# Layer two's projections from scaled float16 halves, with the weights' scale found while layer one runs

## The chip, the cores and the metric

The kernel runs on one core of a Trainium2 chip. A core has engines that run side by side, each through its own list of instructions in order: TensorE (PE, with the load of its stationary operand shown as PEld), VectorE (DVE), ScalarE (ACT), GpSimd (POOL) and SyncE (SP), which here issues the DMA transfers. The metric is the device time of one execution, in microseconds.

## The reference

Two layers over 1024 tokens of width 1024, with 256 memory tokens. Cut to what matters:

```
h = x @ w_in                       # 1024 x 3072: main, memory queries, main gate, memory gate
y_main = main_fn(u_main)           # layer one: pooling in four groups; layer two: forgetting attention, 16 heads
y_mem  = memory_attention(q_mem)   # 4 heads into the memory tokens
y = concat([y_main * silu(g_main), y_mem * silu(g_mem)])
x = layer_norm(ALPHA * x + y @ w_out)
...
h = x @ w_kv_shared                # between the layers: keys, values and forget logits of the attention
logit[t,s] = q_t.k_s/sqrt(64) + cum[t] - cum[s], causal
```

All inputs and the output are float32.

## The kernel before

**Split products.** Every operand is kept as a high and a low part, and a product is three matmuls: high x high, and the two cross products (`three`). High parts are fp32r, which PE takes as f32; low parts are bf16, and so are the operands of both cross products. `hi_lo` makes the parts: ACT casts the high part (L189), DVE subtracts it to get the low one (L190), and a third copy gives the high part in bf16, unless it is read in place as every second bf16 of the f32 tile (`in_place`, L200 with its neighbours, used for weights).

**Slabs.** A projection is worked by `slab`: one slab is 1024 x 128 of a weight matrix, times x turned (width on the partitions), for all 1024 tokens. The weights come in two pieces of 128 x 512 (256 KB; SP loads them into `raw`, a ring of four buffers, and the parts go into rings of four, `w` and `wl`). There are two accumulators, one for each half of the tokens, in banks of a two-bank ring `pj`; for each, 8 products are high x high and 16 cross, 48 matmuls of 512 columns in all, at L253. Layer one has 24 slabs of w_in, layer two 24 of w_in, 8 of the keys and 6 of the values; the first values and the forget logits are 64 x 3 matmuls of 272 columns in `v_first`. The very first slab starts while x is still arriving: its weights are at hand (`ready`), and for each eighth of the width it takes both halves of the tokens in turn.

**Order of work.** PE's instructions are in the order of the program, written by hand. The other engines' lists are ordered by a scheduler. SP issues the transfers in the order of its list and waits at each for its buffer and for one of eight semaphores.

**Layer one.** Four pool groups (`pool_group`); the memory attention lies between group 0 and group 1. A group has two slabs for the values, window sums on DVE (L704 to L710), two slabs for the gates (ACT L283, DVE L284) and four short accumulations of six matmuls with the pool's own weights (PE L231) in a ring `L` of three banks. DVE's L736 multiplies each by its gate, and the result `Y` goes to DRAM (`y0d`).

**Output projection.** `OutProj.rest` takes the tokens in four steps of 256 (`sp`), each in three passes over a third of the mixed width (`c`): SP loads the third as `T` from `y0d`, ACT and DVE split it, PE does 48 matmuls at L540. After the third pass `norm` adds the residual (x rows into `G`), normalises and stores. `turned_rows` turns the rows for layer two: ACT scales them into float16 (hi), DVE gives the rest (lo), SP turns both with a DMA transpose, and ACT L351, DVE L352 and POOL L353 scale them back into f32 and bf16 parts.

**Layer two.** The memory attention and the attention loop `fox`: for each of the heads, 8 tiles of logits (PE L231, a group of three matmuls), DVE L986 adds the forget terms from `R` and takes the maximum, ACT the exponentials, PE the values. POOL masks the diagonal block of `R` ahead of DVE (the select, L978). PE's spare room is filled with the slabs of the pairs of heads to come (`Fill`). In this loop ACT and DVE are left the attention's work, and POOL splits the weights (`low`): L199 makes the high part, L200 the low one, for 54 pieces. `late_gate` does the gates of three pairs late: their slab runs in the loop, and then POOL multiplies the pair's result, loaded back into `R`, by the gate in four products (L1082) and SP stores it.

## Time and profile before

| | |
|---|---|
| median of 3 runs | 1200.42 us (1200.19 to 1201.05) |
| the profiled execution | 1202.12 us |
| its span | 1200.3 us |
| mean granted TensorE clock | 0.997 |
| PE busy | 1182.0 us, 98% |
| DVE, ACT, POOL busy | 800.9, 616.4, 208.3 us |
| DMA queue of the kernel | 180.81 MB, 61.9% of 16 engines' span |

The profile comes from one execution, whose own time stands beside its span; the runs were timed without it. Rows of groups read: line, engine, operation, result<-inputs by the program's names, shape, count | busy us, mean ns of one | idle time of the engine just before, and what ended it. Rows of a timeline begin with the start and the time busy in us. A matmul's end is modelled and overlaps the next one's start, so the time of a matmul in a stream is the distance of two starts, not its duration.

### The profile page before, as it was taken

How to read it: one execution, taken by the hardware profiler on the slowest of the kernel's cores; microseconds unless marked ns; L12 is line 12 of the kernel's file. 1: busy time of each engine (PE TensorE's matmuls, PEld its weight loads, DVE VectorE, ACT ScalarE, POOL GpSimd, SP SyncE). 2: the span in 40 equal slices, each digit the busy share in tenths (PEclk: the TensorE clock that was granted, in tenths of full speed). 3: DMA queues.
4: the chain of work that ended last, by engine and by line, in shares of the span. 5: the costliest groups of instructions: out<-in, count | busy, mean ns of one | idle time of the engine just before them, and what ended most of it. 6: DMA issues, size and time to landing. Idle time of an engine off the chain costs nothing. (4 is left out here: it accounts for less than half of the span.)

```text
span 1200.3 us, 19589 instructions
## 1 busy us (share of the span) xinstructions
PE 1182.0 (98%) x6927; PEld 739.8 (62%) x6927; DVE 800.9 (67%) x1864; ACT 616.4 (51%) x1330; POOL 208.3 (17%) x312
## 2 busy tenths in 40 slices
PE   9999999999999999999999999999999999999997
PEld 4566665555555555677776666666666666655554
DVE  6644766474656676377546888778878888784653
ACT  6433664261532224366325777767766787673110
POOL 2000000000000000200103334343334324530000
PEclk9999999999999999999999999999999999999999
DMA  6333654242265567355526789979997999977431
GB/s 237 110 102 89 137 118 152 85 123 80 92 206 158 158 150 167 106 133 103 173 54 158 153 196 175 194 157 192 189 183 169 192 199 202 228 199 230 157 113 49
DMA packets 280804, 182.06 MB, mean 152 GB/s; under 512 B 225025, under 2 KB 238977, under 8 KB 280705
## 3 DMA queue, kind: packets, MB, share of 16 engines
q1 hardware_dynamic: 280704, 180.81, 61.9%
q8 instruction: 54, 0.88, 0.3%
q14 instruction: 46, 0.37, 0.1%
HBM read 95.24 MB, written 22.61 MB: 98 GB/s over the span
## 5 line engine op out<-in xcount | busy, mean ns | idle before, releaser
L253 PE MATMUL pj<-A,w 128*128 128x512 bf16 (+1 forms) x1888 | 593.9, 398 | 2.7 <-ACT A L189 1.6
L253 PE MATMUL pj<-A,wl 128*128 128x512 bf16 x944 | 357.5, 380 | 0.0
L253 PEld LDWEIGHTS pj<-A,w 128*128 128x128 f32 x944 | 174.9, 189 | 46.5 <-ACT A L189 2.2
L253 PEld LDWEIGHTS <-w 128*128 128x128 bf16 x960 | 92.7, 98 | 120.4 <-issue 38.3
L253 PEld LDWEIGHTS <-wl 128*128 128x128 bf16 x960 | 94.3, 98 | 89.2 <-issue 4.8
L994 ACT ACTIVATE T<-MK,s 128x512 f32<-128x512 f32 x192 | 111.0, 578 | 46.7 <-DVE s L986 24.4
L1015 ACT ACTIVATE P<-T,s 128x512 f16<-128x512 f32 x192 | 102.9, 576 | 52.3 <-issue 25.8
L1016 DVE SCALAR_TENSOR_TENSOR P<-T,s,P 128x512 f16<-128x512 f32 x192 | 112.3, 612 | 24.0 <-ACT P L1015 22.3
L540 PEld LDWEIGHTS <-T 128*128 128x128 bf16 x736 | 70.6, 98 | 88.8 <-issue 6.5
L190 DVE TENSOR_TENSOR wl<-raw,w 128x512 bf16<-128x512 f32 (+1 forms) x96 | 67.8, 712 | 74.3 <-ACT w L189 71.6
L231 PE MATMUL L<-B,B 128*128 128x512 f32 (+3 forms) x384 | 109.2, 387 | 5.7 <-DVE s L986 5.3
L189 ACT CAST w<-raw 128x512 fp32r<-128x512 f32 (+1 forms) x104 | 62.8, 609 | 86.0 <-PE pj L253 64.7
L231 PEld LDWEIGHTS L<-B,B 128*128 128x128 f32 x384 | 71.1, 189 | 31.0 <-DVE s L986 11.3
L353 POOL TENSOR_SCALAR A<-A 128x1024 bf16<-128x1024 f32 x8 | 8.4, 1046 | 447.0 <-ACT A L351 430.3
L978 POOL TENSOR_SCALAR_AFFINE_SELECT R<-R 128x128 f32<-128x128 f32 x128 | 41.9, 333 | 210.0 <-DVE s L986 164.5
L986 DVE CUSTOM_DVE_ANT_0 MK<-L,R 128x512 f32<-128x512 f32 (+3 forms) x128 | 72.8, 568 | 8.0 <-PE L L231 5.6
L200 POOL TENSOR_TENSOR wl<-raw,w 128x512 bf16<-128x512 f32 x54 | 69.3, 1283 | 3.8
L190 DVE TENSOR_TENSOR T<-T,T 128x1024 bf16<-128x1024 f32 x23 | 31.7, 1378 | 46.1 <-ACT T L189 46.0
L189 ACT CAST T<-T 128x1024 fp32r<-128x1024 f32 x23 | 24.1, 1048 | 70.4 <-DMA T<-y1d 45.5
L199 POOL TENSOR_SCALAR w<-raw 128x512 fp32r<-128x512 f32 x54 | 35.7, 661 | 58.7 <-PE pj L253 58.7
L540 PE MATMUL L<-B,T 128*128 128x512 bf16 (+1 forms) x168 | 43.6, 391 | 0.0
L433 ACT ACTIVATE P<-L,s 128x256 f32<-128x256 f32 x64 | 29.6, 473 | 23.3 <-issue 13.0
(296 smaller groups left out, 1793.9 us busy)
## 6 DMA issues: line engine op xcount, KB each, us to landing
raw<-in_win_dram SPq DMA_DIRECT2D x94, 256.0 KB, 2.9
raw<-in_wout_dram SPq DMA_DIRECT2D x40, 256.0 KB, 3.0
B<-B SPq DMA_DIRECT2D x32, 256.0 KB, 4.6
R<-cumd SPq DMA_DIRECT2D x16, 512.0 KB, 4.5
T<-y0d SPq DMA_DIRECT2D x12, 512.0 KB, 4.8
y0d<-Y SPq DMA_DIRECT2D x11, 512.0 KB, 2.7
T<-y1d SPq DMA_DIRECT2D x11, 512.0 KB, 4.7
raw<-in_wmk_dram SPq DMA_DIRECT2D x16, 256.0 KB, 2.7
```

The costliest lines, as they stand in the source:

```text
L189: pin(nc.scalar.copy(hi, src))
L190: pin(by.tensor_tensor(lo[0], src, hi.bitcast(F32), ALU.subtract))
L199: nc.gpsimd.tensor_scalar(hi, src, 1.0, 1.0, ALU.mult, ALU.mult)
L200: nc.gpsimd.tensor_tensor(lo[0], src, hi.bitcast(F32), ALU.subtract)
L231: nc.tensor.matmul(acc, a, b, start=i == 0, stop=i == len(terms) - 1)
L253: nc.tensor.matmul(acc, a, b, start=start, stop=stop)
L540: nc.tensor.matmul(acc, y, w, start=c == 2 and j == firsts[id(acc)] and acc is not self.seeded, stop=c == 1 and j == lasts[id(acc)], skip_ ...
L978: nc.gpsimd.affine_select(R[:, qs], R[:, qs], [[-1, P]], ALU.is_ge, -NEG, base=0, channel_multiplier=1).ins
L986: nc.vector.tensor_tensor_reduce(p[:, lo:up], lg, R[:, lo:up], 1.0, top, ALU.add, ALU.min, m[:, n : n + 1])
L994: nc.scalar.activation(e, p[:, lo:up], AF.Exp, bias=top, scale=-1.0, accum_out=sums[:, n, hd % 2, i : i + 1],)
L1015: nc.scalar.activation(pair[:, lo:up], e, AF.Copy, scale=r)
L1016: nc.vector.scalar_tensor_tensor(pair[:, L + lo : L + up], e, r, pair[:, lo:up], ALU.mult, ALU.subtract)
```

## The change

Six parts, which belong together:

1. x of layer two is kept as two float16 halves (`Tiled`), scaled by a power of two, in blocks of 128 tokens; a slab's matmul takes four such blocks as its moving operand. `turned_rows` ends with the DMA transposes, which write the halves straight into place. L351, L352 and L353 are gone.
2. The weights of layer two's slabs and of `v_first` are scaled by one power of two and split into float16 halves (`split_f16`). All three matmuls of a product are float16. The scales are undone in the operations that empty the accumulators, which were there before.
3. The scale is found in layer one. `look_over` loads all 38 slabs (512 KB each) and the four pieces of `v_first` once more and takes the largest magnitude of each with one DVE reduction; 16 go through the ring `W` in the first two pool groups, 26 through eight slots of a buffer `A` that x of layer one leaves free, in `rest`. The maximum over the partitions goes through DRAM (`weight_scale`).
4. Where POOL splits weights, a multiplication by the scale (L226) comes ahead of the two operations (L227, L228).
5. The first slab takes the three products of the first half of the tokens, then those of the second, for the first two eighths of the width.
6. The four products of a late gate are queued (`lates`) and taken one per tile of logits, two per tile once the last head is under way.

```diff
+class Tiled:
+    def __init__(self, t):
+        self.t = t
+    def at(self, kt, cols):
+        a, b = cols.start // P, cols.stop // P
+        hi, lo = (self.t[:, e, a, kt, :] if b == a + 1 else self.t[:, e, a:b, kt, :] for e in range(2))
+        return hi, (lo, hi)
...
+    def split_f16(src, make):
+        t = make()
+        hi, lo = t[:, 0], t[:, 1]
+        if low[0]:
+            nc.gpsimd.tensor_tensor(src, src, wscale[0].to_broadcast([P, src.shape[1]]) if len(src.shape) == 2 else wscale[0].unsqueeze(2).to_broadcast(list(src.shape)), ALU.mult)
+            nc.gpsimd.tensor_scalar(hi, src, 1.0, 1.0, ALU.mult, ALU.mult)
+            nc.gpsimd.tensor_tensor(lo, src, hi, ALU.subtract)
+        else:
+            nc.scalar.activation(hi, src, AF.Copy, scale=wscale[0])
+            nc.vector.scalar_tensor_tensor(lo, src, wscale[0], hi, ALU.mult, ALU.subtract)
+        return hi, (lo, hi)
+    def w_f16():
+        return sb([P, 2, 4, P], "w", 4, F16)
+    def split_wide(src_dram, make):
+        r = raw([P, 4, P])
+        nc.sync.dma_start(r, src_dram)
+        return split_f16(r, make or w_f16)
...
+        split = split_wide if tiled else lambda src, make: split_w(src, [P, 4, P], make=make or wt)
...
+            nc.tensor.matmul(acc.rearrange("p (s t) -> p s t", t=P) if tiled else acc, a, b, start=start, stop=stop)
...
-                for i in range(3):
-                    for n in range(2):
-                        put(accs[n], *both[n][i], kt == 0 and i == 0, kt == KT - 1 and i == 2)
+                turns = [(i, n) for i in range(3) for n in range(2)]
+                for i, n in sorted(turns, key=lambda t: t[1]) if kt < 2 else turns:
...
+                    if look[0] and len(homes) < 2:
+                        seen[0] = acc
+                        next(look[0], None)
...
-    def turned_rows(z, rows, scale, XH, XL, half, whole):
-        sc, un = scale
-        hi, lo = (half() for _ in range(2))
-        nc.scalar.activation(hi, z, AF.Copy, scale=sc)
-        nc.vector.scalar_tensor_tensor(lo, z, sc, hi, ALU.mult, ALU.subtract)
-        t = whole()
-        nc.sync.dma_start_transpose(t[:, :KT, :], hi)
-        nc.sync.dma_start_transpose(t[:, KT:, :], lo)
-        nc.scalar.activation(XH[:, :, rows], t[:, :KT, :], AF.Copy, scale=un)
-        nc.vector.tensor_scalar(XL[0][:, :, rows], t[:, KT:, :], un, None, ALU.mult)
-        nc.gpsimd.tensor_scalar(XL[1][:, :, rows], XH[:, :, rows].bitcast(F32), 1.0, 1.0, ALU.mult, ALU.mult)
+    def turned_rows(z, tile_of, sc, X, half):
+        for e in range(2):
+            t = half()
+            if e == 0:
+                hi = t
+                nc.scalar.activation(hi, z, AF.Copy, scale=sc)
+            else:
+                nc.vector.scalar_tensor_tensor(t, z, sc, hi, ALU.mult, ALU.subtract)
+            nc.sync.dma_start_transpose(X.t[:, e, tile_of], t)
...
+    def look_over():
+        parts = [(win[1, n], 8 * P) for n in range(24)] + [(wk[n], 8 * P) for n in range(8)]
+        parts += [(wv[n], 8 * P) for n in range(6)] + [(wv0[n], 2 * FW) for n in range(4)]
+        landed = []
+        def reduced():
+            n, t = landed.pop(0)
+            nc.vector.tensor_reduce(tops[:, n : n + 1], t, AX.X, ALU.max, apply_absolute_value=True)
+        for n, (src, cols) in enumerate(parts):
+            t = homes[-1]()[:, :cols]
+            if n < 4:
+                nc.scalar.copy(t[:, :1], seen[0][:, :1])
+            if cols == 8 * P:
+                nc.sync.dma_start(t.rearrange("p (c k) -> p c k", c=2), src.rearrange("c p k m -> p c (k m)"))
+            else:
+                nc.sync.dma_start(t, src.rearrange("p k m -> p (k m)"))
+            landed.append((n, t))
+            if len(landed) > 2:
+                reduced()
+            yield
+        while landed:
+            reduced()
+        m = tiny(1)
+        nc.vector.tensor_reduce(m, tops[:, : len(parts)], AX.X, ALU.max)
+        nc.sync.dma_start(topd.rearrange("a p -> p a"), m)
...
+    def weight_scale():
+        row, m, e, sc = sb([P, P], "raw", 4), tiny(1), tiny(1), wscale[0][:, 6:7]
+        nc.sync.dma_start(row, topd[0].partition_broadcast(P))
+        nc.vector.tensor_reduce(m, row, AX.X, ALU.max)
+        nc.vector.tensor_scalar(m, m, 2.0 ** -100, None, ALU.max)
+        nc.vector.tensor_scalar(e.bitcast(I32), m.bitcast(I32), 0x7F800000, None, ALU.bitwise_and)
+        nc.vector.reciprocal(sc, e)
+        nc.vector.tensor_scalar(sc, sc, 2.0 ** 14, None, ALU.mult)
+        return e
...
+                if look[0] and sp == 3 and c == 2:
+                    run(look[0])
+                    look[0] = None
+                    scales(weight_scale())
...
+                if look[0] and sp < 3:
+                    for _ in range(4):
+                        next(look[0], None)
...
+            if g == 1:
+                homes.append(lambda: sb([P, S], "W", 4, F32, in0))
+                look[0] = look_over()
             pool_group(g)
+            if g == 2:
+                homes.append(None)
             out_proj.split((4, 12, 12)[g - 1])
-        XH1, XL1 = xs()
-        turns = out_proj.rest(x, XH1, XL1, x1)
+        X1 = Tiled(sb([P, 2, ST, KT, P], "A", 2, F16))
+        spare, turn_of = sb([P, 8, S], "A", 2), []
+        def aside():
+            turn_of.append(0)
+            return spare[:, len(turn_of) % 8]
+        homes.append(aside)
+        turns = out_proj.rest(x, X1, None, x1)
...
-            for c in range(4):
+            def product(c):
                 cols = slice(c * 2 * P, (c + 1) * 2 * P)
                 nc.gpsimd.tensor_tensor(o[:, cols], o[:, cols], g[:, cols], ALU.mult)
-            nc.sync.dma_start(y1d[pr // 4][:, pr % 4, :], o)
+                if c == 3:
+                    nc.sync.dma_start(y1d[pr // 4][:, pr % 4, :], o)
+            lates.extend((lambda c=c: product(c)) for c in range(4))
...
+                    for _ in range(min(1 if hd < HEADS else 2, len(lates))):
+                        lates.pop(0)()
```

DVE at the end of pool group 1, before (gates L284, splits of weights L190, evacuations L736):

```order
L190 TENSOR_TENSOR wl_2428<-raw_2425,w_2427 128x512 [waits DMAHW2_49,PE_49,Activation_49]
L190 TENSOR_TENSOR wl_2434<-raw_2431,w_2433 128x512 [waits DMAHW3_49,PE_49,Activation_49]
L284 SCALAR_TENSOR_TENSOR Y_2216<-Y_2216,pj_2256 128x512 [waits Activation_49]
L736 SCALAR_TENSOR_TENSOR Y_2149<-L_2283,pschalf,Y_2149 128x512 [waits DVE_49,PE_49]
L736 SCALAR_TENSOR_TENSOR Y_2149<-L_2291,pschalf,Y_2149 128x512 [waits DVE_49,PE_49]
```

And after (reductions L432 of looks in the ring `W`, splits L203, gate L324, evacuations L839):

```order
L432 TENSOR_REDUCE tops<-W_2497 128x1 [waits DMAHW7_49]
L432 TENSOR_REDUCE tops<-W_2526 128x1 [waits DMAHW0_49]
L203 TENSOR_TENSOR wl_2462<-raw_2459,w_2461 128x512 [waits DMAHW2_49,PE_49,Activation_49]
L432 TENSOR_REDUCE tops<-W_2593 128x1 [waits DMAHW2_49]
L324 SCALAR_TENSOR_TENSOR Y_2238<-Y_2238,pj_2281 128x512 [waits Activation_49]
L839 SCALAR_TENSOR_TENSOR Y_2165<-L_2311,pschalf,Y_2165 128x512 [waits PE_49]
L203 TENSOR_TENSOR wl_2468<-raw_2465,w_2467 128x512 [waits DMAHW5_49]
L839 SCALAR_TENSOR_TENSOR Y_2165<-L_2319,pschalf,Y_2165 128x512 [waits DVE_49,PE_49]
```

All 16 looks of the ring `W` have moved into this stretch; 13 of their reductions stand ahead of the first evacuation.

DVE at the beginning of the output projection, before: the last gate (L284), the four evacuations of the last pool group (L736), then the split of output weights. `Y` are the gated results, `L` the banks.

```order
L190 TENSOR_TENSOR wl_3083<-raw_3088,w_3080 128x512 [waits DMAHW7_49,PE_49]
L284 SCALAR_TENSOR_TENSOR Y_2974<-Y_2974,pj_3014 128x512 [waits Activation_49]
L736 SCALAR_TENSOR_TENSOR Y_2907<-L_3041,pschalf,Y_2907 128x512 [waits PE_49]
L736 SCALAR_TENSOR_TENSOR Y_2907<-L_3049,pschalf,Y_2907 128x512 [waits DVE_49,PE_49]
L736 SCALAR_TENSOR_TENSOR Y_2974<-L_3058,pschalf,Y_2974 128x512 [waits DVE_49,PE_49]
L736 SCALAR_TENSOR_TENSOR Y_2974<-L_3066,pschalf,Y_2974 128x512 [waits DVE_49,PE_49]
```

The same place after (gate L324, evacuation L839, reduction L432 of a look in buffer `A`):

```order
L203 TENSOR_TENSOR wl_3135<-raw_3140,w_3132 128x512 [waits DMAHW7_49,PE_49]
L432 TENSOR_REDUCE tops<-A_3128 128x1 [waits DMAHW6_49]
L324 SCALAR_TENSOR_TENSOR Y_3026<-Y_3026,pj_3066 128x512 [waits Activation_49]
L839 SCALAR_TENSOR_TENSOR Y_2959<-L_3093,pschalf,Y_2959 128x512 [waits PE_49]
L432 TENSOR_REDUCE tops<-A_3128 128x1 [waits DMAHW7_49]
L839 SCALAR_TENSOR_TENSOR Y_2959<-L_3101,pschalf,Y_2959 128x512 [waits DVE_49,PE_49]
L432 TENSOR_REDUCE tops<-A_3128 128x1 [waits DMAHW1_49]
L839 SCALAR_TENSOR_TENSOR Y_3026<-L_3110,pschalf,Y_3026 128x512 [waits DVE_49,PE_49]
```

One reduction, which waits for its load, stands ahead of the last gate, and two stand among the evacuations. SP at the same place, before and then after (L582 and L678 load `T`, L737 and L840 store `Y`, L439 is a look):

```order
L582 DMA T_3174<-y0d 128x4x256
L495 DMA raw_3124<-in_wout_dram 128x512
L737 DMA y0d<-Y_2907 128x1024
L582 DMA T_3227<-y0d 128x4x256
L737 DMA y0d<-Y_2974 128x1024
```

```order
L678 DMA T_3226<-y0d 128x4x256
L439 DMA A_3128<-in_win_dram 128x2x512 x2
L591 DMA raw_3176<-in_wout_dram 128x512
L439 DMA A_3128<-in_win_dram 128x2x512 x3
L840 DMA y0d<-Y_2959 128x1024
L678 DMA T_3287<-y0d 128x4x256
L840 DMA y0d<-Y_3026 128x1024
```

Five looks stand ahead of the first store and of the second load of `T`. POOL in the attention loop, before and then after, with the splits of two pieces between selects (L978, then L1096):

```order
L978 AFFINE_SELECT R_7322<-R_7322 128x128 [waits DMAHW3_49]
L199 TENSOR_SCALAR w_7746<-raw_7744 128x512 [waits DMAHW6_49,PE_49]
L200 TENSOR_TENSOR wl_7747<-raw_7744,w_7746 128x512 [waits PE_49,Pool_49]
L199 TENSOR_SCALAR w_7758<-raw_7756 128x512 [waits DMAHW1_49,PE_49]
L200 TENSOR_TENSOR wl_7759<-raw_7756,w_7758 128x512 [waits PE_49,Pool_49]
```

```order
L1096 AFFINE_SELECT R_7383<-R_7383 128x128 [waits DMAHW7_49]
L226 TENSOR_TENSOR raw_7931<-raw_7931,unrow 128x512 [waits DMAHW4_49,Pool_49]
L227 TENSOR_SCALAR w_7807<-raw_7805 128x512 [waits PE_49]
L228 TENSOR_TENSOR w_7807<-raw_7805,w_7807 128x512 [waits Pool_49]
L227 TENSOR_SCALAR w_7819<-raw_7817 128x512 [waits PE_49]
L228 TENSOR_TENSOR w_7819<-raw_7817,w_7819 128x512 [waits Pool_49]
L1096 AFFINE_SELECT R_7383<-R_7383 128x128 [waits DVE_49]
```

The multiplication of a piece to come (L226) now stands between a select and the two splits, and waits for that piece's load. POOL at the first late gate, before and then after:

```order
L1082 TENSOR_TENSOR R_11733<-R_11733,G_11734 128x256 [waits DMAHW2_49,DVE_49]
L1082 TENSOR_TENSOR R_11733<-R_11733,G_11734 128x256
L1082 TENSOR_TENSOR R_11733<-R_11733,G_11734 128x256 [waits DVE_49]
L1082 TENSOR_TENSOR R_11733<-R_11733,G_11734 128x256
L978 AFFINE_SELECT R_11630<-R_11630 128x128 [waits DVE_49] x3
```

```order
L1201 TENSOR_TENSOR R_11794<-R_11794,G_11795 128x256 [waits DMAHW6_49,DVE_49]
L1201 TENSOR_TENSOR R_11794<-R_11794,G_11795 128x256
L1096 AFFINE_SELECT R_11691<-R_11691 128x128 [waits DVE_49]
L1201 TENSOR_TENSOR R_11794<-R_11794,G_11795 128x256 x2
L1096 AFFINE_SELECT R_11691<-R_11691 128x128 [waits DVE_49] x2
```

A select now stands between the first two products and the last two.

97 lines of the change are left out of this document (60 added, 37 removed).

## The prediction

> **What bounds the kernel now.** I read the page's head, then the waits of PE, then the timeline and the windows at the places where the change takes work away or adds it.
>
> ```profile
> span 1200.3 us, 19589 instructions
> PE 1182.0 (98%) x6927; PEld 739.8 (62%) x6927; DVE 800.9 (67%) x1864; ACT 616.4 (51%) x1330; POOL 208.3 (17%) x312
> ```
>
> PE is busy for 98% of the span, the next engine for 67%. What PE waits for, by releaser (total, times, longest):
>
> ```profile
> PE L L231 <- DVE s L986: 5.3, 10, 1.1
> PE pj L253 <- ACT A L189: 1.6, 1, 1.6
> ```
>
> So there is nothing large to win by removing waits. Time comes down if matmuls get shorter, and goes up if a wait is created. ±2.4 us, 0.2%, is about what a measurement of this kernel can tell from no change.
>
> **Shorter matmuls (the gain).** A slab is 48 matmuls of 512 columns, 16 of them f32 and 32 of 16 bits. PE's timeline over two whole slabs of layer one (start, busy):
>
> ```profile
> 295.65 0.38 PE L253 MATMUL pj<-A,wl 128*128 128x512 bf16 x1
> 295.68 3.34 PE L253 MATMUL pj<-A,w 128*128 128x512 f32 x13
> 298.85 0.38 PE L253 MATMUL pj<-A,wl 128*128 128x512 bf16 x1
> ...
> 301.87 0.38 PE L253 MATMUL pj<-A,wl 128*128 128x512 bf16 x1
> 301.90 1.51 PE L253 MATMUL pj<-A,w 128*128 128x512 f32 x5
> 303.25 0.38 PE L253 MATMUL pj<-A,wl 128*128 128x512 bf16 x1
> ...
> 306.30 3.34 PE L253 MATMUL pj<-A,w 128*128 128x512 f32 x13
> ...
> 316.91 0.58 PE L253 MATMUL pj<-A,w 128*128 128x512 f32 x1
> ```
>
> The pattern repeats after 10.62 and 10.61 us, so a slab takes 10.615 us. From 298.85 to 301.87 there are 14 steps between bf16 starts: 0.2157 us each. 48 of those are 10.354 us, so f32 costs a slab 0.261 us. The two blocks confirm it: (3.20 - 0.216)/13 = 0.2295 and (1.38 - 0.216)/5 = 0.2328 us, which is 12 ns for each f32 matmul and some 25 ns for each block's borders. Float16 in the trace so far:
>
> ```profile
> 567.62 0.83 PE L231 MATMUL T<-T,MK 128*128 128x128 f16 x12
> L231 PE MATMUL T<-T,MK 128*128 128x128 f16 x288 | 20.1, 219 | 0.0
> ```
>
> (0.83 - 0.219)/11 = 55.5 ns for 128 columns, 222 ns for four times as many against 216: a float16 product is no slower than bf16. No row has a moving operand of four blocks of 128; I price it at the 216 of one block, with 222 as the dear end (38 x 48 x 6.3 ns = 11.5 us, more than the gain). 38 slabs x 0.261 = 9.9 us. The 64 f32 products of 272 columns in v_first give 64 x 14.5 ns x 272/512 = 0.5. Against that, in the attention loop the filler's f32 blocks (a third of its products) today often touch the f32 logits of L231; then all borders are open: 128 groups x 1/3 x 25 ns = 1.1 back. **Sum -9.3**, between -10.4 and, with four-block operands at 222 ns, +2.2.
>
> Removed beside PE: eight ACT copies L351, eight DVE scalings L352, eight POOL copies L353 in the turn of the rows. PE has no wait at the border of the layers, so I take 0.
>
> **First slab by halves of the tokens.** PE's start:
>
> ```profile
> 6.72 1.10 PE L253 MATMUL pj<-A,w 128*128 128x512 f32 x3 [1.61 <-ACT A L189]
> ```
>
> The 1.61 us wait is for ACT's half of x. Doing the three products of the first half ahead gives up to three matmuls (0.65 us) to fill it with, if their low halves are there. I take -0.3, from -0.65 to +0.3.
>
> **Late gate's products one per tile.** POOL's timeline, then PE's:
>
> ```profile
> 1036.83 2.81 POOL L1082 TENSOR_TENSOR R<-R,G 128x256 f32<-128x256 f32 x4 [2.23 <-DMA R<-y1d]
> 1039.59 0.29 POOL L978 TENSOR_SCALAR_AFFINE_SELECT R<-R 128x128 f32<-128x128 f32 x1
> 1044.14 0.50 PE L231 MATMUL L<-B,B 128*128 128x256 f32 x2 [1.12 <-DVE s L986]
> ```
>
> Four products keep the next select waiting, DVE's logits wait for the select, and the longest wait of PE follows. After, two stand ahead of it. That wait is the ceiling of the gain; the store of the gated tile, which comes later, is the risk. I take -0.7, from -1.1 to +1.
>
> **The search, pool group 1.** 16 loads of 512 KB, 16 reductions on DVE. The nearest reduction, and DVE's share of that stretch (us, then busy of PE, PEld, DVE, ACT, POOL; clock; DMA share; GB/s):
>
> ```profile
> L332 DVE TENSOR_REDUCE s<-MK 128x1 f32<-128x1024 f32 x6 | 7.3, 1216 | 0.0
> 185.00:235.00 50.00, 50.00 (x228) 28.03 (x227) 28.88 (x44) 19.35 (x31) 0.00 (x0) 1.00 0.38 125
> ```
>
> 16 x 1.216 = 19.5 us; DVE goes from 28.9 to 48.3 of 50. By the order, 13 of the 16 stand ahead of the first pool evacuation, and the weights' low halves stand between them. DVE's idle just holds them, so what decides is bunching: the evacuation may come up to 4.5 us late, the three L banks then hold PE up for some 2.5 us. I take +1, from 0 to +4.
>
> **The search, the beginning of the output projection.** DVE there, the DMA queue of 325 to 345 us (packets, MB, share of the 16 engines) and its loads of T, and two T tiles from DVE to PE:
>
> ```profile
> 324.15 0.69 DVE L284 SCALAR_TENSOR_TENSOR Y<-Y,pj 128x512 f32<-128x512 f32 x1 [1.66 <-ACT Y L283]
> 324.87 0.75 DVE L736 SCALAR_TENSOR_TENSOR Y<-L,pschalf,Y 128x512 f32<-128x512 f32 x1
> q1 hardware_dynamic: 2833, 5.59, 82.5%
> T<-y0d SPq DMA_DIRECT2D x3, 512.0 KB, 5.2
> 334.28 1.37 DVE L190 TENSOR_TENSOR T<-T,T 128x1024 bf16<-128x1024 f32 x1 [1.50 <-ACT T L189]
> 339.33 1.03 PE L540 MATMUL pj<-W,T 128*128 128x512 bf16 x4
> 340.56 1.36 DVE L190 TENSOR_TENSOR T<-T,T 128x1024 bf16<-128x1024 f32 x1 [0.91 <-ACT T L189]
> 349.94 0.62 PE L540 MATMUL pj<-MK,T 128*128 128x512 f32 x2
> ```
>
> After the change a reduction stands ahead of this last gate (L284, then L324), and its load is issued only when PE has left the A buffer at about 323.5. With the 5.2 us to landing of T's loads, as large, or half of that on an idle queue, DVE reaches the gate at 326 to 329 instead of 324.15. The fourth pool accumulation needs the first bank that L736 empties, so PE waits for 1 to 4 us. The stores of Y and the two T loads that read them move with it, behind five looks on SP. Today the T of the second pass is split 3.7 us before PE turns to it (335.65, 339.33), that of the third 8.0 us before (341.92, 349.94). I take +2, from 0 to +6.
>
> **The search, the rest of it.** 26 looks in all, in three steps of 32 us:
>
> ```profile
> 323.50:355.40 31.90, 31.90 (x145) 18.59 (x145) 17.42 (x25) 14.88 (x22) 0.00 (x0) 1.00 0.66 222
> 355.40:387.40 32.00, 32.00 (x146) 18.34 (x145) 19.95 (x31) 7.94 (x9) 2.09 (x2) 1.00 0.54 149
> 387.40:419.30 31.90, 31.90 (x145) 18.27 (x144) 19.57 (x31) 7.93 (x9) 2.09 (x2) 1.00 0.55 149
> ```
>
> The loads of 325 to 345 us are 5.59 MB in 20 us at a share of 0.825: 280/0.825 = 340 GB/s when full. A look is then 1.54 us of all DMA engines, 26 are 40 us, and the idle of the three steps is 0.34 x 31.9 + 0.46 x 32 + 0.45 x 31.9 = 40 us. DVE gets 26 x 1.2 = 31 us more on 57 of 96. Both fit on average, with nothing over on DMA. SP issues in order, so x rows and T tiles queue behind looks; but only eight slots hold looks, and a slot is freed by its reduction. I take +1, from 0 to +8. The scale's own way through memory ends some 30 us before layer two: 0.
>
> **The third POOL operation.** In the attention loop each of 54 weight pieces is first multiplied by the scale on POOL:
>
> ```profile
> L200 POOL TENSOR_TENSOR wl<-raw,w 128x512 bf16<-128x512 f32 x54 | 69.3, 1283 | 3.8
> L978 POOL TENSOR_SCALAR_AFFINE_SELECT R<-R 128x128 f32<-128x128 f32 x128 | 41.9, 333 | 210.0 <-DVE s L986 164.5 <-DVE s L1007 31.0 <-DMA R<-cumd 8.8
> 640.00:850.00 210.00, 207.12 (x1376) 134.71 (x1375) 173.26 (x499) 152.33 (x354) 82.88 (x134) 1.00 0.86 177
> ```
>
> By L200's 1.283 us (two inputs, the same size) that is 69 us more; POOL goes from 82.9 to some 118 of 210 us, 56%. Queued behind it are the selects, then DVE's logits, then the L banks, then PE. 54 operations meet 128 selects; a select that falls behind one is 0.6 us late on the mean, and most have more room than that (PE's 5.3 us of such waits is all there is now). If one piece in ten costs PE a quarter of its length, that is 5.4 x 0.32 = 1.7 us; I take +1.5, from 0 to +8.
>
> Sum: -9.3 - 0.3 - 0.7 + 1 + 2 + 1 + 1.5 = **-4.8**. The profiled execution took 1202.12 us for its span of 1200.3, so it would take 1197.3; against the median of 1200.42 the forecast is 1195.6.
>
> [...] DVE and POOL side by side in the trace:
>
> ```profile
> 699.63 1.27 DVE L1016 SCALAR_TENSOR_TENSOR P<-T,s,P 128x512 f16<-128x512 f32 x2
> 703.19 1.28 POOL L200 TENSOR_TENSOR wl<-raw,w 128x512 bf16<-128x512 f32 x1
> 703.29 1.14 DVE L1016 SCALAR_TENSOR_TENSOR P<-T,s,P 128x512 f16<-128x512 f32 x2
> ```
>
> Two L1016 with POOL idle took 1.27 us, two inside an L200 took 1.14, and that L200 its usual 1.28: neither held the other up. As a rival, if a POOL operation did hold DVE for its length, DVE would be at 173.3 + 35 = 208 of 210 us in this window and some 0.3 us of each of 54 would reach PE, 16 us: 1206. [...]
>
> **The rivals.** (A) Looks and POOL work are all hidden: 1200.4 - 9.3 - 1 = 1190. For it: averages fit everywhere; against it: three queues in which they stand ahead of what PE needs. (B) Slower: the looks' loads hold the output projection's loads up. It decides from 12.7 us of PE wait on (10.3 gained, 2.4 margin). At the 149/0.54 = 276 GB/s of the second step, in place of 340, a look is 1.9 us and 26 are 49 us, 9 more than is idle, and the spare of 3.7 and 8.0 us is taken already by the late stores; with the bank wait of 4 that makes 13, and the first pool group's 2.5 comes from the same loads: 1200.4 - 10.3 + 15.5 = 1205.6. Against it: the looks are limited to eight slots and DVE must empty them, which spaces them out. (C) POOL holds DVE, as above: 1206. (D) Four-block operands take away the gain: 1200.4 + 2.2 - 1 + 5.5 = 1207.
>
> **How the numbers follow.** Forecast with part of the losses (1191 to 1198) 0.43; A (below 1191) 0.16; losses that just eat the gain (1198 to 1202.8) 0.14; B 0.19; C 0.03; D 0.05. Faster is forecast and A, 0.59; within 0.2% 0.14; slower 0.27. The range leaves out the best of A and the worst of B to D: 1187 to 1207; the forecast's own is 1191 to 1198.
>
> **What would show it.** Right: layer two's slabs come at 10.36 us without f32 rows; the gate's products (L1082, then L1201) in pairs and no wait of 1.1 us after it; PE's waits before 320 us and from 323 to 420 us together under 5 us; waits on the logits in the attention loop under 8 us. Wrong: PE rows waiting for ACT or DVE on T tiles from 340 to 420 us (B), L1016 longer than 748 ns on the mean (C), a slab of more than 10.4 us (D).

## The result: slower by 38 us

The changed kernel takes 1238.66 us (median of 4 runs, 1236.78 to 1240.90) against 1200.31 us for the kernel before in the same comparison (1199.42 to 1201.05). The ratio is 1.0321, with a 95% interval of 1.0308 to 1.0334. The forecast was 1195.6 us, with a range of 1187 to 1207. Of all executions in this document one, of the eleven of e10_hold_4, took 2453.61 us and is left out of its ratio.

The profiled execution of after took 1238.05 us, with a span of 1236.3 us. The head of its page:

```profile
span 1236.3 us, 19589 instructions
PE 1181.9 (96%) x6873; PEld 693.6 (56%) x6927; DVE 845.6 (68%) x1908; ACT 612.4 (50%) x1318; POOL 246.1 (20%) x358
```

PE is as busy as before (1181.9 against 1182.0 us) although its matmuls became shorter, and DVE has 45 us more work, POOL 38. PE's waits of after, by releaser (total, times, longest):

```profile
PE L L266 <- DVE s L1104: 26.2, 21, 2.8
PE L L636 <- DVE G L714: 4.1, 1, 4.1
PE L L266 <- DVE Y L839: 2.5, 1, 2.5
PE pj L290 <- DVE B L476: 2.5, 1, 2.5
PE O L1163 <- DMA T<-P: 2.1, 2, 1.9
PE L L636 <- ACT T L202: 1.9, 1, 1.9
```

The first row is the attention loop's and was 5.3 us (L231 waiting for L986). The others are new: two in the output projection (L636), one in pool group 1 (`Y`, L839), one at the beginning of layer two (`B`, L476), one in the loop. The span cut at PE's starts of the same work, from the timelines of both profiles, in us:

| stage | before | after | difference |
|---|---|---|---|
| start to the pool products of group 1 | 227.4 | 225.2 | -2.2 |
| from there to those of group 2 | 47.9 | 52.1 | +4.2 |
| from there to the output projection | 53.4 | 53.4 | 0.0 |
| output projection of layer one | 127.3 | 137.9 | +10.6 |
| from there to the first logits | 183.9 | 184.9 | +1.0 |
| attention loop | 417.4 | 439.4 | +22.0 |
| from there to the end | 143.0 | 143.5 | +0.5 |

Each stage begins with PE's first matmul of its work; the output projection ends with its last. The first row is no gain. The profiled execution of before had a late start (1202.12 us against a median of 1200.3). In the runs called e10 and e13 below, whose first slab is that of before, the same place comes at 225.1 to 225.6. So the loss to be explained is 38 us: 22 in the loop, 16 in layer one and at the border of the layers.

**A wait is not all that a wait costs.** PE's timeline after the wait in pool group 1:

```profile
232.03 1.58 PE L266 MATMUL L<-T,MK 128*128 128x512 bf16 x6 [2.50 <-DVE Y L839]
233.41 2.36 PE L290 MATMUL pj<-A,w 128*128 128x512 f32 x5
235.56 0.63 PE L290 MATMUL pj<-A,wl 128*128 128x512 bf16 x1
235.99 0.63 PE L290 MATMUL pj<-A,w 128*128 128x512 bf16 x1
236.42 0.52 PE L290 MATMUL pj<-A,wl 128*128 128x512 bf16 x1
236.77 0.38 PE L290 MATMUL pj<-A,w 128*128 128x512 bf16 x1
236.99 0.38 PE L290 MATMUL pj<-A,wl 128*128 128x512 bf16 x1
```

From 235.56 to 236.42 the starts are 0.43 us apart, from 236.77 on 0.22. The window of those microseconds shows the clock that was granted, as a share of the full one (the column after POOL's):

```profile
233.29:236.68 3.39, 3.39 (x9) 1.64 (x9) 3.39 (x4) 0.00 (x0) 0.00 (x0) 0.50 0.94 331
```

For 3.4 us PE ran at half the clock, which costs it half of that time, 1.7 us, on top of the 2.50 us of waiting. The same follows the waits that begin at 394, 479, 817 and 994 us; behind the one at 432 us the half clock lasts for 6.8 us, of which PE works for 5.4. That is 11 us in all, over a quarter of the loss; before has none between 11.1 us and the end of PE's last matmul at 1192.6. Of the nine waits of 1.89 to 4.1 us, six have such a stretch behind them; of those under 1.89 us, none has. What tells the six from the other three is shown under "What a wait of a given length costs".

### The profile page after: what moved, and what is told of

The parts are those of the page before. It is cut to its first block, busy times and chain, and to the rows that moved or that the text cites. A ratio compares the mean times of both kernels' runs of the same rounds, so it can differ in the third digit from the quotient of the medians.

```text
span 1236.3 us, 19589 instructions
## 1 busy us (share of the span) xinstructions
PE 1181.9 (96%) x6873; PEld 693.6 (56%) x6927; DVE 845.6 (68%) x1908; ACT 612.4 (50%) x1318; POOL 246.1 (20%) x358
## 5 line engine op out<-in xcount | busy, mean ns | idle before, releaser
L290 PE MATMUL pj<-A,w 128*128 128x512 f16 (+2 forms) x2441 | 631.4, 387 | 1.3 <-DVE B L1011 1.1
L290 PEld LDWEIGHTS <-w 128*128 128x128 f16 (+1 forms) x2112 | 192.0, 98 | 234.3 <-issue 31.2
L266 PE MATMUL L<-B,B 128*128 128x512 f32 (+3 forms) x384 | 118.4, 407 | 26.3 <-DVE s L1104 26.2
L290 PE MATMUL pj<-A,wl 128*128 128x512 bf16 x365 | 137.9, 380 | 2.0 <-ACT A L209 0.6
L1112 ACT ACTIVATE T<-MK,s 128x512 f32<-128x512 f32 x192 | 111.0, 578 | 47.9 <-DVE P L1134 25.3
L1134 DVE SCALAR_TENSOR_TENSOR P<-T,s,P 128x512 f16<-128x512 f32 x192 | 112.3, 612 | 23.8 <-ACT P L1133 22.3
L636 PEld LDWEIGHTS <-T 128*128 128x128 bf16 x736 | 70.8, 98 | 90.2 <-issue 8.6
L203 POOL TENSOR_TENSOR wl<-raw,w 128x512 bf16<-128x512 f32 x8 | 10.2, 1276 | 500.7 <-ACT w L202 497.9
L203 DVE TENSOR_TENSOR wl<-raw,w 128x512 bf16<-128x512 f32 (+1 forms) x78 | 55.4, 719 | 51.7 <-ACT w L202 49.9
L202 ACT CAST w<-raw 128x512 fp32r<-128x512 f32 (+1 forms) x86 | 51.9, 608 | 71.4 <-PE pj L290 49.6
L226 POOL TENSOR_TENSOR raw<-raw,unrow 128x512 f32<-128x512 f32 x54 | 57.5, 1067 | 124.4 <-DMA raw<-in_win_dram 42.8
L290 PEld LDWEIGHTS pj<-A,w 128*128 128x128 f32 x368 | 69.0, 190 | 18.6 <-issue 0.9
L203 DVE TENSOR_TENSOR T<-T,T 128x1024 bf16<-128x1024 f32 x23 | 31.9, 1385 | 55.0 <-ACT T L202 54.9
L228 POOL TENSOR_TENSOR w<-raw,w 128x512 f16<-128x512 f32 x54 | 64.1, 1187 | 3.3
L1096 POOL TENSOR_SCALAR_AFFINE_SELECT R<-R 128x128 f32<-128x128 f32 x128 | 40.2, 320 | 122.3 <-DVE s L1104 111.6
L290 PEld LDWEIGHTS <-wl 128*128 128x128 bf16 x384 | 37.8, 98 | 37.9 <-issue 0.7
L636 PE MATMUL L<-B,T 128*128 128x512 bf16 (+1 forms) x163 | 46.4, 415 | 6.3 <-DVE G L714 4.1
L1104 DVE CUSTOM_DVE_ANT_0 MK<-L,R,s 128x512 f32<-128x512 f32 (+1 forms) x64 | 37.2, 581 | 13.1 <-POOL R L1096 10.3
```

Of the source, the lines that this page charges most:

```text
L202: pin(nc.scalar.copy(hi, src))
L203: pin(by.tensor_tensor(lo[0], src, hi.bitcast(F32), ALU.subtract))
L226: nc.gpsimd.tensor_tensor(src, src, wscale[0].to_broadcast([P, src.shape[1]]) if len(src.shape) == 2 else wscale[0].unsqueeze(2).to_broadc ...
L228: nc.gpsimd.tensor_tensor(lo, src, hi, ALU.subtract)
L266: nc.tensor.matmul(acc, a, b, start=i == 0, stop=i == len(terms) - 1)
L290: nc.tensor.matmul(acc.rearrange("p (s t) -> p s t", t=P) if tiled else acc, a, b, start=start, stop=stop)
```

## The experiments

### The attention loop: the third POOL operation

In after, POOL's list in the loop stands at the loads of the weights. POOL's longest waits for loads and for DVE from 640 to 1060 us, then DVE's for POOL:

```profile
POOL R L1096 <- DVE s L1104: 104.5, 43, 6.4
POOL raw L226 <- DMA raw<-in_win_dram: 41.9, 22, 4.3
POOL raw L226 <- DMA raw<-in_wk_dram: 29.0, 11, 5.6
POOL raw L226 <- DMA raw<-in_wv_dram: 24.8, 9, 5.0
```

```profile
DVE MK L1104 <- POOL R L1096: 23.2, 15, 5.1
```

The multiplication L226 stood at its load 42 times, for 95.7 us together; before, no POOL operation of the split waited for a load. DVE's wait for the selects rose from 2.7 to 23.2 us. One instance, on POOL and then on DVE and PE:

```profile
930.87 1.16 POOL L228 TENSOR_TENSOR w<-raw,w 128x512 f16<-128x512 f32 x1
937.55 1.04 POOL L226 TENSOR_TENSOR raw<-raw,unrow 128x512 f32<-128x512 f32 x1 [5.51 <-DMA raw<-in_wk_dram]
938.54 0.29 POOL L1096 TENSOR_SCALAR_AFFINE_SELECT R<-R 128x128 f32<-128x128 f32 x1
```

```profile
938.87 0.62 DVE L1104 CUSTOM_DVE_ANT_0 MK<-L,R,s 128x384 f32<-128x384 f32 x1 [1.77 <-POOL R L1096]
```

```profile
944.26 0.50 PE L266 MATMUL L<-B,B 128*128 128x256 f32 x2 [2.84 <-DVE s L1104]
```

POOL is idle for 5.51 us with a select queued behind the multiplication, which needs only `R`. DVE needs the select, and PE waits for 2.84 us after that. Between the last two rows DVE also waits for ACT twice (0.81 and 0.93 us), so the rows don't tell how much of the 2.84 us is this one select's. Two theories: it is the waiting (W), or it is the length of the operation, 54 times some 1.07 us (L).

**e1_no_mul** takes L226 out and sets the scale to one; the search runs, but its answer is not used. In the code here `<scale>` and `by` stand for the scale, repeated along the row.

```diff
-            nc.gpsimd.tensor_tensor(src, src, <scale>, ALU.mult)
...
-        nc.vector.tensor_scalar(sc, sc, 2.0 ** 14, None, ALU.mult)
+        nc.vector.tensor_scalar(sc, sc, 0.0, 1.0, ALU.mult, ALU.add)
+        nc.vector.tensor_scalar(e, e, 0.0, 2.0 ** 14, ALU.mult, ALU.add)
```

> The change without the multiplication L226 on POOL; weights are split unscaled (the scale that is found is replaced by one, so the search runs as before and its result is not used). Both theories of the attention loop (W: L226 waits for its load with the selects queued behind it; L: its 57.5 us of work delay the selects) expect the loop's loss of some 27 us back: about 1210 us, PE's waits for DVE s in the loop 5 us instead of 26. [...]

**e3_wait_no_mul** keeps the operation, its wait and its place in POOL's list, but on a single column; the scale is one, as in e1.

```diff
-            nc.gpsimd.tensor_tensor(src, src, <scale>, ALU.mult)
+            one = src[:, 0, :1] if len(src.shape) == 3 else src[:, :1]
+            nc.gpsimd.tensor_tensor(one, one, wscale[0], ALU.mult)
...
```

> L226 stays at its place in POOL's list and reads and writes one column of the piece in place of 512: it still waits for the piece's load, but takes under 0.2 us. Weights unscaled. W expects nearly the whole loss to stay: 1233 to 1239 us. L expects the loss to go: about 1211.

**e9_mul_late** computes the same result with the operation that waits for PE's buffer ahead, as in the kernel before: the scaled high part goes straight into the ring `w`, and `raw` is scaled after it.

```diff
-            nc.gpsimd.tensor_tensor(src, src, <scale>, ALU.mult)
-            nc.gpsimd.tensor_scalar(hi, src, 1.0, 1.0, ALU.mult, ALU.mult)
+            nc.gpsimd.tensor_tensor(hi, src, by, ALU.mult)
+            nc.gpsimd.tensor_tensor(src, src, by, ALU.mult)
             nc.gpsimd.tensor_tensor(lo, src, hi, ALU.subtract)
```

> The change with the three POOL operations of a piece kept together, behind PE's release of the piece's home: the high half straight from the piece by a scaled copy, the multiplication in place after it, then the low half. Same result, POOL's work a little longer (3 x 1.1 us a piece), no operation that waits for a load ahead of a select. W: most of what waiting costs comes back, 1238.7 - 9 = 1230 or better. L: POOL's length decides, so 1238 to 1245.

Measured, with the loop's length and PE's wait for `s` from each profile:

| kernel | us, median | ratio to before (95%) | loop | PE waits for `s` |
|---|---|---|---|---|
| after | 1238.66 | 1.0321 (1.0308 to 1.0334) | 439.4 | 26.2 |
| e3_wait_no_mul | 1223.67 | 1.0196 (1.0166 to 1.0227) | 428.6 | 16.8 |
| e9_mul_late | 1225.13 | 1.0207 (1.0193 to 1.0221) | 426.0 | 16.3 |
| e1_no_mul | 1214.55 | 1.0127 (1.0111 to 1.0144) | 415.8 | 10.6 |

L226 costs 1238.66 - 1214.55 = 24.1 us, less than the 28 or so expected of e1. Neither theory alone holds: e3 lies between what W and L gave for it. The wait with almost no work behind it (0.21 us an operation) costs 9.1 us (e3 less e1), and the operation's length on top of that wait 15.0 (after less e3); e3's interval makes that 4 us more or less. POOL's groups in e9:

```profile
L227 POOL TENSOR_TENSOR w<-raw,unrow 128x512 f16<-128x512 f32 x54 | 56.6, 1047 | 47.5 <-DMA B<-B 35.8 <-PE pj L291 11.8
L228 POOL TENSOR_TENSOR raw<-raw,unrow 128x512 f32<-128x512 f32 x54 | 56.5, 1046 | 3.8
```

The waits for weight loads are gone there, and with three two-input operations POOL has more work than in after (271.3 against 246.1 us); still it is 13.5 us faster, as W expected (1230 or better). So the place in the queue decides 13.5 of the 24.1 us, and the length without that wait costs 10.6 (e9 less e1). DVE's wait for the selects from 640 to 1060 us goes with it: 23.2 us in after, 14.0 in e3, 10.3 in e9 and 0.6 in e1. That is how a length of 1.07 us on an engine with room to spare reaches PE: the selects stand behind it, and DVE behind them.

### Layer one: what of the search costs

Theories: the reductions on DVE, the loads, or the path of the maximum through memory (the store `topd` of 128 partitions, four bytes each). SP's timeline in after around that store:

```profile
409.09 0.53 SPq L450 DMA_DIRECT2D topd<-s  x1
409.72 0.38 SPq L705 DMA_DIRECT2D G<-in_x_dram  x1
410.75 0.32 SPq L731 DMA_DIRECT2D x<-G  x1
411.93 11.44 SPq L394 DMA_TRANSPOSE A<-raw  x2
423.42 1.43 SPq L678 DMA_DIRECT2D T<-y0d  x1
```

Two transposes hold SP for 11.44 us, and the next loads of `T` are issued only from 423.42 on. ACT waits for the second of them until 433.15; DVE's split of it and, behind that, the operation that empties PE's bank (L714) come so late that PE stands for 4.1 us (the second row of its waits). The DMA issues of 405 to 425 us (KB each, median us to landing), after and then before at 400 to 425:

```profile
G<-in_x_dram SPq DMA_DIRECT2D x1, 512.0 KB, 12.5
x<-G SPq DMA_DIRECT2D x1, 512.0 KB, 12.7
topd<-s SPq DMA_DIRECT2D x1, 0.5 KB, 9.3
```

```profile
G<-in_x_dram SPq DMA_DIRECT2D x2, 512.0 KB, 4.8
x<-G SPq DMA_DIRECT2D x1, 512.0 KB, 5.6
T<-raw SPq DMA_TRANSPOSE x3, 4.8
```

What is in flight with the store takes some 7 us longer, and the store's own half kilobyte 9.3 us.

**e5_no_search** drops looks, reductions and the way through memory, for a constant maximum of 0.6.

```diff
...
-        nc.sync.dma_start(row, topd[0].partition_broadcast(P))
-        nc.vector.tensor_reduce(m, row, AX.X, ALU.max)
+        nc.vector.memset(m, 0.6)
...
-                    run(look[0])
...
-                look[0] = look_over()
+                look[0] = iter(())
```

> No looks, no reductions, no way through DRAM; the scale is the constant 2^15 from a written maximum of 0.6. The attention loop is as in the change. Expected if the search costs what the stages lost: pool group 1 4.1 us, output projection of layer one 10.6, beginning of layer two about 4, so 1238.7 - 19 = 1220 us. If the search's loads and reductions cost nothing by themselves and only the store of 4-byte elements does: 1231.

**e4_row_store** writes 512 bytes of one partition instead of four bytes of each of 128 (the first partition's maximum, repeated; the others are left out).

```diff
-        nc.sync.dma_start(topd.rearrange("a p -> p a"), m)
+        flat = sb([P, P], "raw", 4)[:1]
+        nc.vector.tensor_scalar(flat, m[:1, :1].to_broadcast([1, P]), 1.0, None, ALU.mult)
+        nc.sync.dma_start(topd, flat)
```

> The 128 maxima are no longer stored as 128 elements of 4 bytes from 128 partitions; one partition's maximum is stored as one row of 512 bytes (the maximum over the other partitions is left out). Theory J (the store of 4-byte elements jams the DMA engines from 410 to 421 us) expects T in the third step to land 8 to 10 us earlier, the wait of 4.3 us near 431 us and the half clock behind it gone: 1231 to 1233 us. The rival, that looks and transposes fill the engines, expects no change: 1238.

**e12_looks_no_reduce** is e4 with a constant maximum, and every reduction reads one column of its look in place of all.

```diff
-            nc.vector.tensor_reduce(tops[:, n : n + 1], t, AX.X, ALU.max, apply_absolute_value=True)
+            nc.vector.tensor_reduce(tops[:, n : n + 1], t[:, :1], AX.X, ALU.max, apply_absolute_value=True)
```

> The change with the row store, all 42 looks loaded, but each reduction reads one column of 1024 in place of all (the found scale is replaced by the constant of 0.6). Compared with the run of the row store alone (1226.7). If the 50 us of reductions on DVE cost pool group 1 its wait and part of the output projection's: 1222. If the loads alone do it, by the x rows and weights that queue behind them: 1226.

**e13_store_alone** puts nothing but such a store (128 partitions, four bytes each, read by nobody) and the copy of one column that it stores into the kernel before, at the same stage.

```diff
+            if s == 3 and XH is not None:
+                m = tiny(1)
+                nc.vector.tensor_scalar(m, r, 1.0, None, ALU.mult)
+                nc.sync.dma_start(topd.rearrange("a p -> p a"), m)
```

> The kernel before, with one store of 128 elements of 4 bytes, one from each partition, into one row of DRAM, in the output projection of layer one (of a norm's factor; its value is not used), where the change stores its maxima. No looks. J (that store by itself jams the DMA engines for some 10 us) expects loads and stores of 4 KB packets issued behind it to take 3 to 9 us a packet, SP's next DMA transpose to stand for some 10 us, the T behind it to be late and the time to rise by 3 to 8 us: 1203 to 1208. If the jam needs the looks too: 1200, and no packet over 2 us there.

| kernel | us, median | ratio to before (95%) | output projection | from there to the logits |
|---|---|---|---|---|
| after | 1238.66 | 1.0321 (1.0308 to 1.0334) | 137.9 | 184.9 |
| e4_row_store | 1226.66 | 1.0231 (1.0204 to 1.0258) | 131.2 | 181.8 |
| e12_looks_no_reduce | 1226.66 | 1.0226 (1.0206 to 1.0247) | 130.6 | 185.0 |
| e5_no_search | 1219.14 | 1.0159 (1.0144 to 1.0174) | 127.3 | 181.1 |
| e13_store_alone | 1208.93 | 1.0074 (1.0057 to 1.0091) | 134.9 | 183.9 |

The search costs 19.5 us (after less e5, which came where it was expected); e4 gained some 5 us more than expected. 12.0 of it go with the form of the store (after less e4) and 7.5 with the loads and the rest of the way through memory (e12 less e5). The reductions, though they are 50 us of DVE, show in no total: e4 less e12 is 0.0, as expected if the loads do it (1226, against 1222). But each of these differences can be off by 3 to 4 us. The four runs of e4 span 1224.72 to 1232.47 us, those of e12 1224.02 to 1231.23, and in both the longest has the lowest mean clock (0.991, against 0.995 and 0.996 in the shortest).

The stages tell more. Of the 12.0, 6.7 us are in the output projection and 3.1 behind it. In e4's profile pool group 1 is 2.9 us shorter too; that lies ahead of the store, which can't be its cause. Among the kernels whose work in that stage is the same its wait differs: 2.3 to 2.5 us with a stretch of half clock behind it in after, e3 and e9 (51.9 to 52.1 us for the stage), 2.1 and 1.2 us without one in e1 and e4 (50.0 and 49.2). In the output projection the store's form is plain: with the store of after it takes 135.2 to 137.9 us (after, e1, e3, e9), with the row 131.2 and 130.6 (e4, e12). And in e12, whose reductions read one column, the wait in pool group 1 is gone and the stage takes 47.9 us, as before. So the reductions did cost that wait; in e12's total it does not show, since its start is 1.4 us later and its way to the logits 3.3 us longer than e4's.

The store alone costs the kernel before 8.8 us, a little over what was expected of it. SP and the transposes among the issues of 400 to 425 us in e13:

```profile
398.12 0.53 SPq L622 DMA_DIRECT2D topd<-s  x1
...
402.26 9.84 SPq L351 DMA_TRANSPOSE T<-raw  x1
412.19 0.55 SPq L583 DMA_DIRECT2D T<-y0d  x1
```

```profile
T<-raw SPq DMA_TRANSPOSE x2, 12.3
```

```profile
417.54 1.22 PE L541 MATMUL L<-MK,T 128*128 128x512 f32 x2 [5.87 <-ACT T L189]
```

A transpose that landed after 4.8 us in before takes 12.3, SP stands for 9.84 us, the next `T` is issued at 412.19, and PE waits for 5.87 us. With the row of e4 the transposes beside the store land as in before:

```profile
A<-raw SPq DMA_TRANSPOSE x4, 4.4
```

In the trace's packets from 396 to 415 us, 33 of 271 of 4 KB take 2 to 9.4 us in e13; before, none there took over 2, and in e4 none from 400 to 425 us over 1.2. In after it is 33 of 256 from 405 to 425 us, with 2.2 to 9.6 us. So the runs show that the store holds up the transfers beside it; they don't show the reason.

### What a wait of a given length costs

**e10_hold_4** and **e10_hold_8** make DVE late in the kernel before: 4 or 8 reductions of the first bank `L` of pool group 2 stand ahead of the operation that empties it.

```diff
                     mm3(acc, grouped(terms, n == 1))
+                    for _ in range(4 if g == 2 and d == 0 and n == 0 else 0):
+                        nc.vector.tensor_reduce(tiny(1), acc, AX.X, ALU.max)
```

> The kernel before, with four DVE reductions of the first accumulation's bank ahead of its evacuation in pool group 2 (their results are not used). They start some 0.61 us apart: 2.4 us, of which the fourth accumulation has 1.24 us of room (evacuation ended at 278.06, the fourth begins at about 279.3). PE waits for 1.2 us once. A wait costs its length only: 1200.0 + 1.2 = 1201.2. If a short wait too is followed by a stretch at half clock: 1202.7.

> The same with eight reductions: 4.9 us, a single wait of PE of 3.6 us. If a wait costs its length only: 1203.6. If a wait of over 2 us is followed by about 3 us at half the clock, as the traces of the change show after 229, 394, 431 and 479 us: 1203.6 + 1.5 = 1205.1, with matmuls of 512 columns some 430 ns apart for seven or eight of them.

e10_hold_4: 1201.25 us, 1.0008 (0.9999 to 1.0017), with a wait of 0.85 us. e10_hold_8: 1205.01 us, 1.0042 (1.0028 to 1.0055), which is 5.0 us for this wait:

```profile
281.10 2.72 PE L231 MATMUL L<-T,MK 128*128 128x512 bf16 x6 [3.24 <-DVE Y L738]
283.62 1.38 PE L253 MATMUL pj<-A,w 128*128 128x512 f32 x5
```

Six matmuls take from 281.10 to 283.62, 0.42 us each instead of 0.216. So the wait of 3.24 us cost half as much again as its length; the one of 0.85 us cost 1.3 us (-0.1 to 2.0 by the interval), which is its length within the error. Both totals came where they were expected (1205.1 and 1201.2).

Why some waits are followed by half the clock and others are not can be read from the profiles. In each of the 14 that were kept, all changes of the granted clock lie on one grid of 3.41 us, and what tells the two cases apart is how long PE stood idle within one window of that grid. Three windows of after:

```profile
816.97:820.36 3.39, 1.19 (x10) 0.75 (x10) 3.36 (x9) 1.15 (x4) 0.20 (x1) 1.00 0.73 162
820.38:823.77 3.39, 3.39 (x45) 3.19 (x44) 1.14 (x6) 1.52 (x4) 0.96 (x1) 0.50 1.65 229
939.85:943.24 3.39, 1.57 (x8) 0.76 (x6) 1.93 (x3) 3.10 (x6) 1.29 (x2) 1.00 0.31 88
```

The wait of 2.20 us that ends at 819.22 lies within the first, where PE works for 1.19 us of 3.39, and the next window has half the clock. The longer wait of 2.84 us that ends at 944.26 is cut by the grid: 1.83 us of it lie in the third window and 1.01 in the next, and the full clock stays. Over all 14 profiles, from 20 to 1170 us and at full clock, each of the 24 windows with 2.00 us or more of idle PE was followed by half the clock, and none of the 49 with 1.20 to 1.92 us; of two between, one was (1.95) and one was not (1.98). The longest wait that passed without it is one of 3.91 us in e3, cut into 1.98 and 1.92. In after alone it is six windows with 1.95 to 2.65 us of idle PE, each followed by half the clock, and seven with 1.28 to 1.89 us, none of them followed by it.

### What the gain would be by itself

**e6_neither** joins e1 and e5: no search and no L226, the weights split into unscaled float16 halves. **e7_half_late** is the kernel before with parts 5 and 6 of the change alone (the first slab by halves, the late gate's products one per tile).

> No search and no multiplication on POOL: weights split unscaled into float16 halves, scale one, everything else as changed. If the losses are those two and nothing else, the gains stand alone: 9.3 us from the shorter matmuls, 2.2 from the first slab (PE reaches the first pool accumulation 2.2 us earlier in the change), something under 1 from the late gates: 1188 us, PE without waits over 1.2 us after the start. If the two losses only add up as measured singly (24.1 and 19.5 off 1238.7) it is 1195, and 7 us are still lost somewhere.

> The kernel before with parts 5 and 6 alone: the first slab by halves of the tokens for its first two eighths, the late gates' products one per tile. By the landmark of the first pool accumulation 2.2 us earlier, and up to 1.1 for the late gates: 1197.5 us. If the start's gain is given back before the end (the next waits move up), 1200.

e6_neither takes 1195.85 us, 0.9965 (0.9953 to 0.9978): 4.2 us faster than the kernel before and the fastest here that leaves no product out, but without the protection that a scale found in the weights gives. It came where the two losses only add up (1195). e7_half_late takes 1199.00 us, 0.9990 (0.9981 to 1.0000), between its two expectations. So the float16 products bring 1199.00 - 1195.85 = 3.15 us where 9.3 were counted; in the profiles 2.3 us of it lie between the output projection and the first logits, and 0.2 in the loop. The window of the whole loop (us, then busy time of PE, PEld, DVE, ACT, POOL; clock; DMA share; GB/s), e7 and then e6:

```profile
638.00:1054.00 416.00, 410.38 (x2752) 267.59 (x2752) 340.72 (x975) 302.17 (x699) 162.77 (x261) 1.00 0.91 186
```

```profile
635.50:1051.50 416.00, 404.42 (x2753) 232.38 (x2752) 340.92 (x975) 304.68 (x698) 156.60 (x261) 1.00 0.91 186
```

PE has 6.0 us less to do in the loop, yet the loop is as long (415.7 against 416.0 us). PE's wait for the logits' maximum has grown instead, again e7 and then e6:

```profile
PE L L231 <- DVE s L986: 4.1, 9, 1.0
```

```profile
PE L L265 <- DVE s L1102: 10.4, 15, 1.6
```

**e11_one_less** tests whether shorter matmuls can shorten that loop at all: e7 with one cross product of 48 left out of each of layer two's slabs.

```diff
-                put(acc, a, b, j == 0, j == len(order) - 1)
+                if not (fewer[0] and n == 0 and j == 4):
+                    put(acc, a, b, j == 0, j == len(order) - 1)
...
```

> The kernel with parts 5 and 6 alone, and in each of layer two's 38 slabs one matmul of 48 left out (a cross product, so the output is a little less exact): 0.22 us of PE a slab, about what float16 saves. If PE's work is what bounds the attention loop, the loop falls by 27 x 0.22 = 5.9 us, and the run to 1199.0 - 8.2 = 1190.8. If the loop is bound by the chain of logits through DVE, so that PE's shorter work comes back as waits for DVE s, the loop stays at 415.9 us and only the 11 slabs ahead of it gain: 1196.6, with the loop's waits up by some 5 us.

It takes 1194.03 us, 0.9949 (0.9937 to 0.9962), between the two expectations, and its loop 411.8 us: 4.2 us of the 5.8 that 27 matmuls make (27 x 0.2157). So the loop can be shorter. But e6 and e11 are not alike in another respect. Going by the order of the results' names in the traces, DVE's list in e6's loop has some 20 of 1248 instructions at another place than e7's, and e11's has some 170; ACT's has about 5 and 100 of 845. The scheduler answered to the missing matmuls with another order. Whether e6 returns its gain because DVE's and ACT's order stayed as it was, and would keep it with another, stays open.

## Why the prediction was wrong

The measured differences add up: -1.0 (parts 5 and 6, e7) - 3.15 (float16, e6 against e7) + 24.1 (L226) + 12.0 (store) + 7.5 (loads) = +39.5, against 38.35 measured for the whole. By the prediction's steps:

- **The third POOL operation, +1.5 (0 to 8): 24.1. This step failed, by the most.** It priced the operation by its length, and a select that falls behind one as late by half of that. It named the queue (selects, DVE, L banks, PE) but not what the operation itself waits for, though POOL's list showed that it waits for a load. The high part that stood first on POOL before writes into the ring `w` and waited for PE to free it, at a time when its load had landed (in the loop it waited for PE 14 times and for its load never). L226 works in place on `raw`: it needs nothing but the load, comes as early in POOL's list as that allows, and then stands there, 42 times, with the selects behind it. "One piece in ten costs a quarter of its length" had no row under it. Of the 24.1 us, 13.5 go with that place in the queue; the length alone would still have cost 10.6, a little beyond the step's dear end of 8.
- **"The scale's own way through memory ... 0": the store costs 8.8 by itself (e13) and 12.0 in after (less e4, of which 2.9 lie ahead of it).** The step looked only at when the scale would be ready. That was wrong as well: it is ready at 450.2 us (the last row of L417 on DVE), 18 us ahead of layer two and not 30. But the cost is in what the store does to the transfers around it, and no row of before had a store of four bytes per partition. An operation that no row shows needed a bound from both sides, and a bare zero was taken.
- **The search, +1 +2 +1: 7.5, and not where it was put.** In pool group 1 the mechanism came as described, a wait of 2.5 us for the late evacuation (`Y`, L839), and with the reductions cut to one column (e12) it is gone; the stage lost 4.2, since the half clock came on top. At the beginning of the output projection the wait of 1 to 4 us did not come: from the fourth group's pool products to the first of the projection it is 5.5 us (325.1 to 330.6), as before. The rest cost more than 1: in e12 the projection is 3.3 us longer than in e5, and the way to the logits 4.0.
- **Shorter matmuls, -9.3: -3.15.** The price of a product was right. PE's timeline of a layer-two slab in after:

```profile
520.13 5.34 PE L290 MATMUL pj<-A,P 128*128 128x512 f16 x24
```

With 0.38 us for the last, as the rows above show for one alone, 23 steps take 4.96 us, 0.216 each; four-block operands cost no more, so rival D falls. What failed was the step from PE's work to the time. PE was busy for 98%, but in the loop it and DVE wait for each other in turn, and 6 us came back as waits for DVE. Ahead of the loop 2.3 us came of the 3.4 that the price gives for 11 slabs and `v_first`.
- **First slab and late gates, -0.3 and -0.7: -1.0 together** (0.0 to 2.3 by the interval). The sum came as forecast, but the first slab's part by luck: the 1.61 us wait on which it rested is 0.17 to 0.54 us in e10 and e13, whose first slab is the same, and in e7 the pool products of group 1 come at 225.4, no earlier than there. What came is in the loop, 416.0 us in e7 against 416.9 to 417.7 in before, e10 and e13.
- **Rivals.** A needed everything hidden; e6, which leaves the search and L226 out, shows that even then the time is not 1190 but 1196. B ended on the right side, and its place was right, but of the 10.6 us of the output projection 6.7 go with one small store and not with bandwidth. C's sign did not come: the mean of the 128x512 product (L1016, then L1134) is 748 ns in both kernels, and of the 25 products of any shape that lie wholly within a two-input operation of POOL in after, none took over 753.

```profile
L1134 DVE SCALAR_TENSOR_TENSOR P<-T,s,P 128x512 f16<-128x512 f32 x80 | 58.7, 748 | 13.7 <-ACT P L1133 12.4
```

- **C was set aside on rows of one kind of product.** The two pairs of L1016 have different shapes (512 and 384 columns, 512 and 256), so that their times, 1.27 and 1.14 us, can't be compared; and the kernel takes `T` there from its PSUM banks, so that the product has only one input in SBUF. The loop also has six products with both inputs in SBUF in each kernel (`MK<-MK,s,MK`, 128x1024), and these and POOL's operations did lengthen each other. DVE, then POOL, in before:

```profile
740.31 1.28 DVE L340 SCALAR_TENSOR_TENSOR MK<-MK,s,MK 128x1024 f16<-128x1024 f32 x1
793.34 2.03 DVE L340 SCALAR_TENSOR_TENSOR MK<-MK,s,MK 128x1024 f16<-128x1024 f32 x1 [0.60 <-ACT MK L339]
```

```profile
740.47 1.27 POOL L978 TENSOR_SCALAR_AFFINE_SELECT R<-R 128x128 f32<-128x128 f32 x1 [3.25 <-DVE s L986]
```

  The select that began inside the first took 1.27 us in place of 0.29; the second, which began 0.33 us into a split of POOL (L200), took 2.03 in place of 1.28. With six such operations a kernel this is small here: together they take 10.3 us in after and 9.2 in before.

- **A term that no step had:** the half clock after a wait, 11 us in after's profile. It is part of what the steps above measured, and added 1.7 to 2.7 us to each of six waits.

## What to carry to other kernels

On an engine that works its list in order, ask of each added operation not only how long it takes but what it waits for and what stands behind it: L226, which needs only its load, was placed early, and POOL stood at that load 42 times, for 95.7 us, with the selects behind it. A small store need not be a free one; one of four bytes in each of 128 partitions delayed the transfers beside it (a transpose landed after 12.3 us instead of 4.8), where the same 512 bytes from one partition's row did not (4.4). And where PE alternates with another engine, take from the trace which of the two sets the pace before counting shorter matmuls as time: here 6.0 us less work for PE left the loop at 415.7 us, against 416.0.
